# Moving the rows of the first batch so that each half of its load is one contiguous megabyte

## The chip, the cores and the metric

The kernel runs on one NeuronCore of a Trainium2 chip. In profiles DVE is VectorE, ACT is ScalarE, POOL is GpSimd and SP is SyncE, which here only issues transfers. The time is the device time of a run in microseconds. All ratios below are the mean time of one kernel's fast runs over the mean time of the other's fast runs in the same rounds, so they are not quite the ratios of the medians that stand beside them.

## The reference

A masked softmax over the last axis. Each batch has one length, and columns from that length on become zero.

```python
batch, heads, seq_q, seq_k = 16, 8, 256, 256
x       # float32, 16 x 8 x 256 x 256, 2 MB for each batch
lengths # 128 to 255, one for each batch

for b in range(batch):
    length = lengths[b]
    masked = x[b, :, :, :length]
    masked = masked - np.max(masked, axis=-1, keepdims=True)
    e = np.exp(masked)
    result[b, :, :, :length] = e / np.sum(e, axis=-1, keepdims=True)
```

The rows of a batch are independent of each other and share a length. A row may therefore sit in any partition, as long as it is stored where it came from.

## The kernel before

Each batch is 2048 rows of 1 KB. Partition p holds the 16 rows 16p to 16p + 15, so its share is 16 KB that are contiguous in memory.

```python
x_f = x.rearrange("b h q k -> b (h q) k").rearrange("b (p t) k -> b p t k", p=P)
out_f = ...  # the same for the output
slots, ahead = 8, 4            # 8 batches in SBUF, the first 4 loaded by SP

# SP: batch 0 in two halves (8 of each partition's 16 rows), then batches 1 to 3 whole
for h in range(2):
    s = slice(h * half, (h + 1) * half)
    nc.sync.dma_start(out=xt[:, 0, s], in_=x_f[0, :, s]).then_inc(s_ld[h], 16)
for b in range(1, ahead):
    nc.sync.dma_start(out=xt[:, b], in_=x_f[b]).then_inc(s_ld[b + 1], 16)

# SP: stores, the first not before the third half has been exponentiated
nc.sync.wait_ge(s_exp, 3)
for b in range(batch):
    for s in parts(b):         # batch 0 in one piece, most others in two or three
        nc.sync.wait_ge(s_out, 2 * b + (s.stop - 1) // half + 1)
        # ... (a wait from batch 2 on is cut)
        nc.sync.dma_start(out=out_f[b, :, s, :], in_=xt[:, b % slots, s, :])  # ...

# GpSimd: loads of batches 4 to 15, only the columns that are needed, in a loop
nc.gpsimd.wait_ge(s_ld[ahead - 1], 16)         # batch 2 has landed
# ... wait for the slot's store; pick a width; start the load

# VectorE: clip (the mask) and divide; ScalarE: exp with row sums
def mask(b, s): ...    # waits for the load: for batch 0, for each half by itself
def divide(b, h): ...  # waits for exp; reciprocal, then multiply
mask(0, slice(0, half))
mask(0, slice(half, nt))
```

The softmax here doesn't subtract the row's maximum and nothing guards it: scores larger than these inputs give would overflow.

## Time and profile before

| | before |
|---|---|
| median of 4 runs | 156.16 us (155.84 to 156.23) |
| span in the profile | 154.7 us |
| busy share of DVE / ACT | 75% / 68% |
| time of DMA packets, per DMA engine | 151.4 us |
| DVE's first clip starts at | 6.60 us |
| first store issued at | 19.86 us |

The lines are shown in the prediction. The page gives busy shares and forty slices of the span. The timeline gives start, length, engine, source line and operation of each instruction. The stretches give busy times, the DMA share and the rate in GB/s. A stretch counts a packet whole where it starts, so its rate is rough by a packet for each engine. Beside these, the trace has a record of each DMA packet: its queue, start, size and duration. In SP's queue one packet carries one partition's contiguous run; GpSimd's packets here have 1280 to 16384 B.

The **packet sum** is the time of all packets of both data queues, divided by 16 engines. The **excess** of a transfer is what its packets took over their usual 611 ns (16384 B) or 309 ns (8192 B), summed and divided by 16; where a stretch holds GpSimd's packets, each is compared with what its size usually takes, and only differences between kernels count there. A **landing** is the end of a transfer on one of the 16 engines, and the **spread** is the time between the first landing and the last. The **MB by 24 us** spread each packet's bytes evenly over its time.

The prediction and the expectations count packet times from a zero 0.13 us before that of the timeline, and in the MB by 24 us they count each started packet whole (8.93 MB for the kernel before). The text below uses the timeline's zero.

### The profile page before, as it was taken

How to read it: one execution, taken by the hardware profiler on the slowest of the kernel's cores; microseconds unless marked ns; L12 is line 12 of the kernel's file. 1: busy time of each engine (PE TensorE's matmuls, PEld its weight loads, DVE VectorE, ACT ScalarE, POOL GpSimd, SP SyncE). 2: the span in 40 equal slices, each digit the busy share in tenths (PEclk: the TensorE clock that was granted, in tenths of full speed). 3: DMA queues.
4: the chain of work that ended last, by engine and by line, in shares of the span. 5: the costliest groups of instructions: out<-in, count | busy, mean ns of one | idle time of the engine just before them, and what ended most of it. 6: DMA issues, size and time to landing. Idle time of an engine off the chain costs nothing.

```text
span 154.7 us, 1324 instructions
## 1 busy us (share of the span) xinstructions
PE 0.2 (0%) x1; PEld 0.1 (0%) x1; DVE 115.7 (75%) x84; ACT 105.2 (68%) x514; POOL 19.0 (12%) x25
## 2 busy tenths in 40 slices
PE   0000000000000000000000000000000000000000
PEld 0000000000000000000000000000000000000000
DVE  1249999952999696979979696969689629796700
ACT  3087799992692959778695959595976906959200
POOL 4910031000220110201111020202001000000000
DMA  4999999999999999999999999999999999999992
GB/s 116 426 449 424 428 398 406 398 407 447 400 410 395 402 409 414 415 417 411 404 424 407 417 408 409 415 416 416 416 417 419 419 448 415 426 445 419 430 421 85
DMA packets 9988, 62.08 MB, mean 401 GB/s; under 512 B 850, under 2 KB 946, under 8 KB 6274
## 3 DMA queue, kind: packets, MB, share of 16 engines
q1 hardware_dynamic: 5904, 41.95, 65.8%
q0 software_dynamic: 4080, 20.12, 32.1%
q14 instruction: 2, 0.02, 0.0%
q10 hardware_dynamic: 2, 0.00, 0.0%
HBM read 28.51 MB, written 33.55 MB: 401 GB/s over the span
## 4 chain that ended last, share of the span: by engine, by line
DMA 55%; DVE 19%; ACT 8%; issue 8%; ACTq 2%; SPq 1%; POOLq 1%; DVEq 0%
DMA xt<-in_x_dram 34%; DMA out_dram<-xt 21%; DVE xt L222 9%; DVE xt L195 9%; ACT xt L252 8%; ACTq L252 2%; DVE inv_sum L219 1%; SPq L109 1%; POOLq L99 0%; SPq L111 0%; SPq L120 0%; DVEq L212 0%; POOLq L135 0%; POOLq L130 0%; ACTq L247 0%
## 5 line engine op out<-in xcount | busy, mean ns | idle before, releaser
L252 ACT ACTIVATE xt<-xt x256 | 102.4, 401 | 37.2 <-DVE xt L195 37.2
L222 DVE TENSOR_TENSOR xt<-xt,inv_sum 128x2048 f32<-128x2048 f32 x32 | 73.4, 2292 | 1.1
L252 ACT ACTIVATION_READ_ACCUMULATOR xt<-xt x256 | 47.9, 187 | 0.0
L195 DVE SCALAR_TENSOR_TENSOR xt<-down,len_s,xt 128x2048 f32<-128x2048 f32 (+1 forms) x17 | 37.8, 2222 | 13.1 <-DMA xt<-in_x_dram 13.0
L130 POOL DMA_DIRECT2D xt<-in_x_dram x12 | 12.8, 1064 | 95.5 <-issue 50.6
L219 DVE RECIPROCAL inv_sum<-row_sum 128x8 f32<-128x8 f32 x32 | 6.3, 198 | 14.4 <-ACT xt L252 14.4
L149 POOL MEMSET xt<- 128x1536 f32 x4 | 5.3, 1386 | 1.1 <-DVE len_s L186 1.1
L244 ACT ACT_TABLE_LOAD x1 | 1.3, 1283 | 1.6 <-SPq L81 1.6
L178 DVE TENSOR_SCALAR down<-iota_i 128x256 f32<-128x256 int32 x1 | 0.3, 297 | 1.6 <-POOL iota_i L141 1.6
L183 DVE CAST len_b<-word 1x16 bf16<-1x16 int32 x1 | 0.2, 163 | 0.4 <-DMA word<-in_lengths_dram 0.4
L186 DVE TENSOR_SCALAR len_s<-len_f 128x16 f32<-128x16 f32 x1 | 0.2, 174 | 0.3 <-PE len_f L165 0.3
L141 POOL IOTA iota_i<- 128x256 int32 x1 | 0.3, 331 | 0.6 <-SPq L81 0.6
L146 POOL MEMSET seed<- 1x1 f32 x2 | 0.3, 162 | 0.0
L244 ACT ACTIVATE warm<-const-float32-0.0 128x1 f32<-128x1 f32 x1 | 0.2, 203 | 0.0
L144 POOL MEMSET ones<- 1x128 bf16 x1 | 0.2, 194 | 0.0
L165 PE MATMUL len_f<-len_b,ones 1*128 1x16 bf16 x1 | 0.2, 164 | 2.6 <-DVE len_b L183 2.6
L275 POOL MEMSET const-float32-0.0<- 128x1 f32 x1 | 0.1, 98 | 0.3 <-issue 0.3
L165 PEld LDWEIGHTS len_f<-len_b,ones 1*128 1x128 bf16 x1 | 0.1, 99 | 2.6 <-POOL ones L144 2.6
L275 POOL MEMSET const-float32-1.0<- 128x1 f32 x1 | 0.1, 98 | 0.0
L275 POOL MEMSET const-bfloat16-1.0<- 128x1 bf16 x1 | 0.1, 98 | 0.0
L275 POOL MEMSET const-uint8-127<- 128x1 uint8 x1 | 0.1, 98 | 0.0
L275 POOL BASE_LOAD x1 | 0.0, 17 | 0.1
## 6 DMA issues: line engine op xcount, KB each, us to landing
out_dram<-xt SPq DMA_DIRECT2D x19, 1024.0 KB
out_dram<-xt SPq DMA_DIRECT2D x14, 512.0 KB
xt<-in_x_dram SPq DMA_DIRECT2D x3, 2048.0 KB, 16.1
out_dram<-xt SPq DMA_DIRECT2D x3, 2048.0 KB
xt<-in_x_dram POOLq DMA_DIRECT2D x3, 1728.0 KB, 16.9
xt<-in_x_dram POOLq DMA_DIRECT2D x2, 2048.0 KB, 18.5
xt<-in_x_dram POOLq DMA_DIRECT2D x2, 1600.0 KB, 16.8
xt<-in_x_dram POOLq DMA_DIRECT2D x2, 1280.0 KB, 14.8
```

The costliest lines, as they stand in the source:

```text
L109: nc.sync.dma_start(out=xt[:, 0, s], in_=x_f[0, :, s]).then_inc(s_ld[h], 16)
L130: nc.gpsimd.dma_start(out=xt[:, slot, :, :w], in_=x_n[:, n, :, :w]).then_inc(s_sw[par], 16)
L141: nc.gpsimd.iota(iota_i, pattern=[[1, seq_k]], base=0, channel_multiplier=0).then_inc(s_iota, 1)
L146: nc.gpsimd.memset(seed[:, par : par + 1], 0.0).then_inc(s_st[par], 64)
L149: nc.gpsimd.memset(xt[:, b, :, low:], 0.0).then_inc(s_fill, 1)
L165: nc.tensor.matmul(len_f, lhsT=ones, rhs=len_b, start=True, stop=True).then_inc(s_lenf, 1)
L195: return nc.vector.scalar_tensor_tensor(out=t, in0=down[:, None, lo:hi].to_broadcast([P, s.stop - s.start, hi - lo]), scalar=len_s[:, b : ...
L219: step(nc.vector.reciprocal(out=inv_sum[:, b, s], in_=row_sum[:, b, s]))
L222: nc.vector.tensor_tensor(out=t, in0=t, in1=inv_sum[:, b, s, None].to_broadcast([P, half, seq_k]), op=ALU.mult,).then_inc(s_out, 1)
L244: nc.scalar.activation(out=warm, in_=nc.const_aps.tensor(0.0, (P, 1), F32), func=EXP)
L252: ins = nc.scalar.activation(out=e, in_=e, func=EXP, accum_out=sum_h[:, bass.ds(i, 1), j])
L275: nc = _bacc.Bacc("TRN2", target_bir_lowering=False, num_devices=1)
```

## The change

The intent is an earlier first half. Partition p now holds rows 8p to 8p + 7 of the first megabyte and rows 8p to 8p + 7 of the second, so each half of the load is one contiguous megabyte. The store must put the rows back, so it writes two runs of 8 KB per partition instead of one of 16 KB.

```diff
+    x_0 = x[0].rearrange("h q k -> (h q) k").rearrange("(u p t) k -> p u t k", u=2, p=P)
+    out_0 = out[0].rearrange("h q k -> (h q) k").rearrange("(u p t) k -> p u (t k)", u=2, p=P)
...
-            nc.sync.dma_start(out=xt[:, 0, s], in_=x_f[0, :, s]).then_inc(s_ld[h], 16)
+            nc.sync.dma_start(out=xt[:, 0, s], in_=x_0[:, h]).then_inc(s_ld[h], 16)
...
-                nc.sync.dma_start(
-                    out=out_f[b, :, s, :], in_=xt[:, b % slots, s, :]
-                ).then_inc(s_b, 16 * ((s.stop - s.start) // quarter))
+                if b == 0:
+                    to = out_0
+                    at = xt[:, b, s, :].rearrange("p (u t) k -> p u (t k)", u=2)
+                else:
+                    to = out_f[b, :, s, :]
+                    at = xt[:, b % slots, s, :]
+                nc.sync.dma_start(out=to, in_=at).then_inc(s_b, 16 * ((s.stop - s.start) // quarter))
```

## The prediction

> **What bounds the kernel now.** I read the page's busy shares first, then the queues, then the end of the chain, then the first ten microseconds, because the change touches only the first batch.
>
> Busy shares, the forty slices and the queues of the kernel before:
>
> ```profile
> PE 0.2 (0%) x1; PEld 0.1 (0%) x1; DVE 115.7 (75%) x84; ACT 105.2 (68%) x514; POOL 19.0 (12%) x25
> ...
> DMA  4999999999999999999999999999999999999992
> ...
> DMA packets 9988, 62.08 MB, mean 401 GB/s; under 512 B 850, under 2 KB 946, under 8 KB 6274
> ...
> q1 hardware_dynamic: 5904, 41.95, 65.8%
> q0 software_dynamic: 4080, 20.12, 32.1%
> ```
>
> No compute engine is over 75% busy, and the DMA row is at 9 from the second slice to the last but one. The two queues' packets took 65.8% + 32.1% = 97.9% of 16 engines' span, 0.979 x 154.7 = 151.5 us for each DMA engine. The packets start 2.2 us after the span begins and end near 152, so the DMA engines are never without work. The time is a start of 2.2 us, some 150 us of packets, and a tail of under 3 us in which the last semaphores arrive and the program closes.
>
> The stretches at the end (length; busy time and instruction counts of PE, PEld, DVE, ACT, POOL; clock; DMA share; GB/s):
>
> ```profile
> 20.00:140.00 120.00, 0.00 (x0) 0.00 (x0) 99.11 (x70) 89.68 (x445) 12.77 (x12) 1.00 1.02 414
> ...
> 148.00:150.00 2.00, 0.00 (x0) 0.00 (x0) 0.00 (x0) 0.00 (x0) 0.00 (x0) 1.00 1.05 442
> 150.00:151.00 1.00, 0.00 (x0) 0.00 (x0) 0.00 (x0) 0.00 (x0) 0.00 (x0) 1.00 0.97 410
> 151.00:152.00 1.00, 0.00 (x0) 0.00 (x0) 0.00 (x0) 0.00 (x0) 0.00 (x0) 1.00 0.53 221
> ```
>
> The last division ends at 144.33 + 2.29 = 146.6 us, yet the engines carry on at full rate until about 151.3. That is 4.7 us; the last store is 1 MB, which at 414 GB/s takes 2.5 us. So some 2 us of older stores stood in front of it. The compute chain has about 2 us of slack at the end: the end is set by the sum of packet times. A change counts if it alters that sum, or leaves the engines without work.
>
> Now the beginning (start, length, engine, line, operation):
>
> ```profile
> 1.13 0.86 SPq L109 DMA_DIRECT2D xt<-in_x_dram  x2
> ...
> 6.60 1.28 DVE L195 SCALAR_TENSOR_TENSOR xt<-down,len_s,xt 128x1024 f32<-128x1024 f32 x1 [3.61 <-DMA xt<-in_x_dram]
> ...
> 9.05 1.29 DVE L195 SCALAR_TENSOR_TENSOR xt<-down,len_s,xt 128x1024 f32<-128x1024 f32 x1 [1.16 <-DMA xt<-in_x_dram]
> ...
> 19.86 8.20 SPq L120 DMA_DIRECT2D out_dram<-xt  x4
> ```
>
> The halves of batch 0 reach the DVE 9.05 - 6.60 = 2.45 us apart. A megabyte in 2.45 us is 1.049 MB / 2.45 us = 428 GB/s: the second half already comes at the full rate, with its 8 KB out of every 16 KB. Batch 0's store is issued at 19.86, when the loads of batches 1 to 3 still stand in the queue.
>
> The trace also has a record of each DMA packet. In the SP queue each partition's contiguous run is one packet: 8192 B for the two halves (256 packets), 16384 B for loads and stores of whole batches, 8192 or 4096 B for stores in parts. Their times, on one DMA engine:
> - first 64 packets of batch 0 (four on each engine): mean 457 ns, up to 1275; the other 192: 309 to 318 ns.
> - loads of batches 1 and 2, 16384 B: all 256 of them exactly 611 ns.
> - 8192 B stores later on: medians 309 to 315 ns. All of these write 8 KB out of every 16 KB too.
> - batch 0's store, 128 packets of 16384 B: median 612, mean 651, up to 1140 ns.
>
> **What the Trainium skill says.** Its page "DMA: Bandwidth & Descriptors", section "Bandwidth", part "Where 436 GB/s comes from", puts the ceiling of the 16 engines at 435 GB/s. The trace agrees: 428 GB/s here, 16 x 8192 B / 309 ns = 424, and 16 x 16384 B / 611 ns = 429. There is next to nothing left for a better address pattern. The same section, "Why small descriptors are slow (HBM only)", states a fixed cost of some 3 cycles for a packet. The trace shows one of that kind: 2 x 309 - 611 = 7 ns for one more packet.
> The section "Latency and other measured facts" says that large power-of-two distances between the partitions' rows in HBM cost rate: 207 GB/s per direction at 512 KiB, 164 at 2 MiB, against 214. The new store has runs one megabyte apart, so this bears on it, but within each megabyte the partitions are 8 KB apart; nothing in the trace of before tests it. The section "Queues, rings and completion order" says that an engine takes turns between queues packet by packet, which matters for one rival below.
>
> **The change part by part.**
> 1. Loads. Each half remains 128 runs of 8192 B, spread over the same 16 engines. Only the HBM addresses move: runs one after another instead of every other run. Packets removed or added: none. Expected at 309 ns each: no difference. What could be saved is the slow opening, (457 - 309) x 4 = 592 ns per engine. I think this belongs to starting, not to the stride: the 192 packets after it have the same stride and go at 309, and batches 1 and 2 enter memory never touched before at 611 from the first packet. I put the expected gain at 0.1 us of those 0.59.
> 2. Store. Each partition's 16 KB now goes to two places, so 128 packets of 16384 B become 256 of 8192 B: eight more packets on each engine. At 2 x 309 - 611 = 7 ns per pair, or 2 x 313 - 611 = 15 ns with the later stores' median, it costs 8 x 7 to 8 x 15 ns = 0.06 to 0.12 us per engine. This lies in the sum that sets the end, so it counts in full.
> 3. Issue. The store's instruction describes twice the runs, perhaps a few tenths of a microsecond more on SP (its issues take a median of 374 ns now). It is issued at 19.86, and its first packet starts at 22.67 behind the loads: 2.8 us in which that is hidden.
> 4. Compute. Rows move to other partitions, but all rows of a batch share one length: same instructions, same shapes. Nothing changes.
> Sum: -0.1 + 0.1 = 0, with a few tenths of noise: 156.19 becomes about 156.2.
>
> **The rivals.**
> - The first half comes sooner. For it: the first packets' 457 ns, and that a contiguous megabyte is half the address range. Against it: the even 309 right after. Full success would take 0.59 us off the start; since the engines have work from then on, all of it could reach the end: 155.6, 0.4% faster. It can't make 2%.
> - The store of two streams a megabyte apart runs badly. For it: the skill's row pitches, and batch 0's store already showing some slow packets. Against it: only two such streams, and 16 engines well spread within them. At the skill's loss for 2 MiB, 214/164, the store's 2.10 MB / 414 GB/s = 5.07 us would become 6.6 us: 157.7, still the same. Only half rate, +5.1 us, would make 161 and count as slower. I give that about one chance in a hundred.
> - The queues' turns shift. Batch 4's load, issued by GpSimd at 20.85, had its first packets only from 26.6, when batch 0's store was nearly through, and DVE then sat idle for 4.42 us until 37.62. Store packets of half the size let that load in with smaller steps, so it may land sooner by something like half a microsecond. The DVE's idle time shrinks by as much, but the packets' sum is the same, and the compute has slack at the end: 156.2 again, perhaps 0.2 either way from a different order of stores and loads.
> - The first division and the first store start earlier, so that loads into reused slots are let go earlier. It needs the first rival, and the DMA engines have no gap that it could fill: nothing.
>
> **Range and chances.** The runs of before span 155.84 to 156.23. The small effects add up to between -0.6 and +0.4; another chip or another day may add 0.3. I predict 156.2, with 155.5 to 157.0 for eight in ten. Two per cent is 3.1 us: a gain of that size has no source in a change that touches 4 of 62 MB already at 98% of the engines' peak, and a loss needs the store at about 60% of its rate. Chances: 0.005 faster, 0.98 same, 0.015 slower.
>
> **What would show it right or wrong.** Right: 128 more packets, about 10116; the SP queue's share of the span within 0.3 points of 65.8%; DVE's first clip within 0.3 us of 6.60 and the second 2.4 to 2.5 us after it; packets of batch 0's store at 309 to 315 ns in the median. Step 1 is wrong if the first 64 packets fall well below 457 ns, or the later 192 rise above 309. Step 2 is wrong if the store's packets take over 330 ns in the mean. The whole would be wrong if a gap opened in the DMA row, or if the end followed the last division without the 4.7 us of stores after it: then compute would be the bound, and the first half's landing would count.

## The result, and the profile after

The changed kernel takes 156.29 us in the median of 4 runs (156.15 to 156.57), and the kernel before 156.16. The ratio is 1.0014, with a 95% interval of 0.9994 to 1.0035: the same.

The page of the changed kernel, busy shares, DMA row, packets and queues:

```profile
PE 0.2 (0%) x1; PEld 0.1 (0%) x1; DVE 115.8 (75%) x84; ACT 105.2 (68%) x514; POOL 19.0 (12%) x25
...
DMA  3999999999999999999999999999999999999992
...
DMA packets 10116, 62.08 MB, mean 401 GB/s; under 512 B 850, under 2 KB 946, under 8 KB 6274
...
q1 hardware_dynamic: 6032, 41.95, 65.9%
q0 software_dynamic: 4080, 20.12, 32.1%
```

There are 128 packets more, all in the SP queue. The bytes, the instructions and the shares are otherwise those of before.

Stretches of the changed kernel at the end (columns as in the prediction):

```profile
20.00:140.00 120.00, 0.00 (x0) 0.00 (x0) 98.05 (x70) 88.19 (x437) 12.77 (x12) 1.00 1.02 414
...
150.00:151.00 1.00, 0.00 (x0) 0.00 (x0) 0.00 (x0) 0.00 (x0) 0.00 (x0) 1.00 0.99 418
151.00:152.00 1.00, 0.00 (x0) 0.00 (x0) 0.00 (x0) 0.00 (x0) 0.00 (x0) 1.00 0.83 352
```

The rate in the long middle is 414 GB/s as before, and the transfers run into the 152nd microsecond again. The opening differs, though. The timeline of the changed kernel:

```profile
1.13 0.86 SPq L113 DMA_DIRECT2D xt<-in_x_dram  x2
...
6.24 1.28 DVE L203 SCALAR_TENSOR_TENSOR xt<-down,len_s,xt 128x1024 f32<-128x1024 f32 x1 [3.24 <-DMA xt<-in_x_dram]
8.69 1.28 DVE L203 SCALAR_TENSOR_TENSOR xt<-down,len_s,xt 128x1024 f32<-128x1024 f32 x1 [1.17 <-DMA xt<-in_x_dram]
...
19.53 8.26 SPq L130 DMA_DIRECT2D out_dram<-xt  x4
```

Both halves are clipped 0.36 us earlier than before (6.60 and 9.05), and the first store is issued 0.33 us earlier (19.86). The last division, in the same timeline:

```profile
145.46 2.29 DVE L230 TENSOR_TENSOR xt<-xt,inv_sum 128x2048 f32<-128x2048 f32 x1
```

It ends at 147.8 us, 1.1 us later than before, and the transfers go on after it.

The span has not become shorter. So where did the third of a microsecond go? The stretches around that first store, first of the kernel before:

```profile
20.00:22.00 2.00, 0.00 (x0) 0.00 (x0) 1.97 (x3) 2.00 (x11) 1.15 (x1) 1.00 1.08 418
22.00:24.00 2.00, 0.00 (x0) 0.00 (x0) 1.97 (x3) 2.00 (x11) 0.14 (x1) 1.00 0.92 360
```

and of the changed kernel:

```profile
20.00:22.00 2.00, 0.00 (x0) 0.00 (x0) 1.97 (x3) 2.00 (x11) 1.29 (x1) 1.00 1.11 401
22.00:24.00 2.00, 0.00 (x0) 0.00 (x0) 1.97 (x3) 2.00 (x11) 0.00 (x0) 1.00 0.85 299
```

Both kernels dip here, the changed one deeper. With each packet's bytes spread over its time, the rates from 22 to 24 us are 374 and 328 GB/s, a smaller gap than the stretches' 360 and 299. By 24 us the changed kernel has moved 8.72 MB against 8.85 MB: 0.13 MB, or 0.31 us at 414 GB/s. I then had four things to settle. Is the earlier landing real or luck? Is the deeper dip real, and what makes it? And what is a microsecond at the opening worth at the end?

### The profile page after: what moved, and what is told of

The parts are those of the page before. It is cut to its first block, busy times and chain, and to the rows that moved or that the text cites. A ratio compares the mean times of both kernels' runs of the same rounds, so it can differ in the third digit from the quotient of the medians.

```text
span 154.7 us, 1324 instructions
## 1 busy us (share of the span) xinstructions
PE 0.2 (0%) x1; PEld 0.1 (0%) x1; DVE 115.8 (75%) x84; ACT 105.2 (68%) x514; POOL 19.0 (12%) x25
## 4 chain that ended last, share of the span: by engine, by line
DMA 55%; DVE 20%; ACT 8%; issue 8%; ACTq 2%; SPq 2%; POOLq 1%; DVEq 0%
DMA xt<-in_x_dram 34%; DMA out_dram<-xt 20%; DVE xt L230 10%; DVE xt L203 9%; ACT xt L260 8%; ACTq L260 2%; SPq L130 1%; DVE inv_sum L227 1%; SPq L113 1%; POOLq L103 0%; SPq L115 0%; DVEq L220 0%; POOLq L143 0%; POOLq L138 0%; ACTq L255 0%
```

## The experiments

Twelve kernels ran. The calls' medians of the kernel before, over 11 runs each, were 156.27, 156.02 and 156.05 us. Kernels that change only one side of batch 0 store its rows in a wrong order.

**Theories.** A: the addresses make no difference, and what the two traces show is chance. B: contiguous runs land earlier, and the store gives it back.

### Both kernels again

No edit.

> The kernel before, unchanged, to see how far the opening and the middle move by themselves. Theory A (the addresses make no difference; the 0.36 us by which the first clip came earlier in the changed kernel, and the 0.13 MB by which its DMA engines were behind from 24 us on, are chance): the first clip starts anywhere in 6.2 to 6.7 us, and the bytes moved by 24 us anywhere in 8.7 to 9.0 MB. Theory B (the contiguous load lands earlier, and the store in two pieces gives it back): the first clip at 6.6 again within 0.1, and 8.9 MB moved by 24 us. Ratio 1.000 within 0.002 in both.

> The changed kernel, unchanged. Theory A: as for the kernel before, the first clip anywhere in 6.2 to 6.7 us and 8.7 to 9.0 MB moved by 24 us; ratio 1.000 to 1.001. Theory B: the first clip at 6.24 again within 0.1, the mean of the first 64 packets near 412 ns, 8.74 MB by 24 us; ratio 1.000 to 1.002, since gain and loss cancel.

The kernel before took 156.19 us (ratio 0.9995, 0.9975 to 1.0014) and the changed kernel 156.17 us (ratio 0.9997, 0.9971 to 1.0023). The change is worth nothing that 6 runs can see. The first clip of the kernel before, repeated:

```profile
6.52 1.28 DVE L195 SCALAR_TENSOR_TENSOR xt<-down,len_s,xt 128x1024 f32<-128x1024 f32 x1 [3.53 <-DMA xt<-in_x_dram]
```

and of the changed kernel, repeated:

```profile
6.17 1.28 DVE L203 SCALAR_TENSOR_TENSOR xt<-down,len_s,xt 128x1024 f32<-128x1024 f32 x1 [3.19 <-DMA xt<-in_x_dram]
```

The 0.35 us are there again, and so is the dip: 8.86 MB by 24 us in the kernel before and 8.76 MB in the changed one. Theory A loses its main point.

### The loads alone, and the store alone

```diff
# loads_only and loads_again: the new loads, the store as before
-                if b == 0:
+                if False:
                     to = out_0
# store_only: the loads as before, the new store
-            nc.sync.dma_start(out=xt[:, 0, s], in_=x_0[:, h]).then_inc(s_ld[h], 16)
+            nc.sync.dma_start(out=xt[:, 0, s], in_=x_f[0, :, s]).then_inc(s_ld[h], 16)
```

> Contiguous first loads, the store as before (the rows of batch 0 are then stored in a wrong order; on purpose). Theory A: ratio 1.000 within 0.001, time as before. Theory B: first clip at 6.24, 8.93 MB or more by 24 us, and the 0.2 to 0.4 us of the opening reach the end: ratio 0.9975 to 0.9990.

> First loads as before, batch 0's store in two runs per partition a megabyte apart (wrong order of rows; on purpose). Theory A: eight more packets per DMA engine at 7 to 15 ns, so 0.06 to 0.12 us: ratio 1.0004 to 1.0008. Theory B: first clip at 6.6, a loss of 0.3 to 0.5 us between 22 and 24 us that the load does not make up: ratio 1.002 to 1.003.

> Only the loads changed, a second time (wrong order of rows on purpose). The first try gave 0.9982, 95% interval 0.9962 to 1.0002. The delay of 1.1 us at the first clip cost 0.45 us at the end, so by the same slope 0.33 us gained there would be worth 0.14 us. Theory G (a part of the gain reaches the end): ratio 0.998 to 0.9995. Theory N (nothing reaches it): 0.9995 to 1.001. The first clip at 6.15 to 6.35 us in both.

| kernel | median us | ratio (95%) | first clip, us | MB by 24 us | excess of batch 3's load, us |
|---|---|---|---|---|---|
| loads only | 155.94 | 0.9982 (0.9962 to 1.0002) | 6.23 | 8.74 | 0.53 |
| loads only, again | 156.20 | 1.0002 (0.9987 to 1.0018) | 6.23 | 8.72 | 0.65 |
| store only | 156.23 | 0.9992 (0.9971 to 1.0013) | 6.50 | 8.84 | 0.38 |

The earlier clip comes with the loads. So does the deeper dip, and theory B had put it on the store: B's second half is wrong as stated. The time moves with neither. The first try of the loads alone looked like a gain, the second did not, so any gain is below what these runs resolve, about 0.2%.

The store's own cost is in its packets. Their mean was 331, 325 and 329 ns in the three profiles with the new store and normal timing (changed kernel, its repeat, store only). The packets of 16384 B of batch 0's store took 651 and 642 ns in the two profiles of the kernel before. With sixteen small packets against eight large ones per engine, that is 16 x 331 - 8 x 651 = 88 ns, and 16 x 325 - 8 x 642 = 64 ns for the repeats. In the two kernels of the next section but one, where no load of GpSimd runs beside this store, the means are 309.0 and 611.0 ns: 16 x 309 - 8 x 611 = 56 ns. The median small packet took 309 ns, the same as in a load, so two streams a megabyte apart do no harm.

### Runs farther apart

```diff
+    x_w = x[0:2].rearrange("b h q k -> (b h q) k").rearrange("(p t) k -> p t k", p=P)
-            nc.sync.dma_start(out=xt[:, 0, s], in_=x_f[0, :, s]).then_inc(s_ld[h], 16)
+            nc.sync.dma_start(out=xt[:, 0, s], in_=x_w[:, s]).then_inc(s_ld[h], 16)
```

> The kernel before, with each partition of the first two loads taking 8 KB out of every 32 KB (rows of batch 1 among them, so batch 0's output is wrong on purpose). In the six profiles so far the spread of the 16 engines' landings of the first half was 0.90, 0.78, 0.74 us with 8 of 16 KB and 0.46, 0.24, 0.34 us with contiguous runs; the mean landing was 5.57 to 5.64 us in all six. Theory B1 (the distance between runs makes some engines lose more than others in the first rounds): spread 0.7 us or more and the first clip at 6.5 or later. Theory A1 (what helps is only that a contiguous megabyte starts alike on all engines by some other chance): spread anywhere from 0.2 to 0.9, first clip 6.1 to 6.7.

> Runs of 8 KB out of every 32 KB, a second time (wrong on purpose), now timed. The first look had the first clip at 6.14 us and a spread of 0.44 us. If the distance of 16 KB is what is bad: first clip under 6.4 and spread under 0.7 again, and a time like that of the contiguous loads, 0.997 to 0.9995. If the first look was luck: first clip 6.5 or later.

The single look took 155.81 us (state unknown), the timed repeat 155.97 us (ratio 0.9992, 0.9979 to 1.0006). The clip in the first look:

```profile
6.14 1.28 DVE L197 SCALAR_TENSOR_TENSOR xt<-down,len_s,xt 128x1024 f32<-128x1024 f32 x1 [3.16 <-DMA xt<-in_x_dram]
```

In the repeat it came at 6.20. The spread of the landings was 0.44 and 0.52 us, and the mean landing 5.29 and 5.30 us, earlier than in any other kernel (5.44 to 5.55). So a greater distance between runs is not worse, and theory B1 falls: contiguity isn't what makes the last landing early. Of the three patterns tried, it is 8 KB out of every 16 KB whose last engine lands late. Why that one does, and what other distances do, no run shows.

### GpSimd's first load held back

GpSimd's instruction for batch 4's load begins at 20.4 to 20.9 us and lasts 1.3 us, just where the dip is, so it was a suspect.

```diff
         nc.gpsimd.wait_ge(s_ld[ahead - 1], 16)
+        nc.gpsimd.wait_ge(s_ld[ahead], 16)
```

> The kernel before, with GpSimd's first load held until batch 3 has landed (about 24 us instead of 18.8). Theory P (the slow packets at 21 to 23 us come from GpSimd's descriptor writing for batch 4's load, which starts at 20.5 to 20.9): the excess over the packets' floor between 20 and 24 us falls from 0.35 us per engine to under 0.1. Theory W (they come from the change from reads to writes, when the first store's packets enter): it stays at 0.3 or more. Time within 0.3 us of the kernel before in both, since batch 4's load did not move before 26.6 us anyway.

> The changed kernel with the same hold. Theory P: excess between 20 and 24 us falls from 0.63 us per engine to under 0.15, bytes moved by 24 us rise from 8.76 to 8.9 MB or more, batch 3's mean landing from 23.27 to 23.0 us. Theory W: 0.5 us or more stays, and 8.7 to 8.8 MB. Time within 0.3 us of the kernel before in both.

GpSimd's first load in the kernel before with the hold:

```profile
26.97 1.29 POOL L130 DMA_DIRECT2D xt<-in_x_dram  x1 [18.60 <-issue]
```

GpSimd is now far from the dip, but the excess between 20 and 24 us stays: 0.38 us with the old loads (0.35 and 0.38 without the hold) and 0.61 us with the new ones (0.64 and 0.65). Theory P is wrong for that stretch. It was right about a smaller piece: between 24 and 28 us, the excess of 0.24 and 0.17 us of the kernel before went to 0.00. It came back later, where the held load now was: 0.7 us more between 28 and 36 us than in the kernel before.

My expectation for the time was wrong. The holds took 157.07 us (1.0066, 1.0048 to 1.0083) and 157.42 us (1.0085, 1.0064 to 1.0106). I had argued that batch 4's load didn't move before 26.6 us anyway. But it had to wait behind what SP had queued before it. Issued at 26.97 instead of 20.85, its first packet came at 32.3 instead of 26.5, and batch 4's clip at 41.41 instead of 37.62.

### The first clip delayed

The 0.34 us can be taken the other way: let the landing be as it is, and delay the clip with a VectorE operation into a spare tile.

```diff
+        nc.vector.wait_ge(s_ld[0], 16)
+        for r in range(1):       # slow_1us: 1 x 128x1024; slow_4us: 2 x 128x2048
+            dn = down[:, None, :].to_broadcast([P, 4, seq_k])
+            nc.vector.tensor_tensor(out=spare[:, r], in0=dn, in1=dn, op=ALU.max)
         mask(0, slice(0, half))
# after_delayed: the same in the changed kernel, 1 x 128x256
```

> The kernel before with one more VectorE operation of about 1.2 us (128x1024) between the landing of the first half and the first clip: three times the 0.34 us that the change gained there, in the other direction. Theory S (the first landing is not on the path, because the first store's packets come 2.8 us after its issue behind the loads): the first clip 1.2 us later, the first store issued near 21.0 instead of 19.86, the first packet of it still at 22.7, time within 0.2 us of the kernel before, ratio 0.999 to 1.001. Rival R (each microsecond at the opening is one at the end): ratio 1.006 to 1.008.

> The kernel before with two VectorE operations of about 2.3 us each (128x2048) before the first clip, so some 4.4 us of delay. Theory S (there is slack of about 1.6 us, the 2.8 us between the first store's issue and its first packet less the 1.2 us that a store takes from issue to packet; past it every microsecond counts): 4.4 - 1.6 = 2.8 us, ratio 1.016 to 1.020. Theory L (a steady 0.4 us for each microsecond, as the smaller delay showed): 1.8 us, ratio 1.010 to 1.013. Rival R (all of it): 1.027 to 1.029.

> The changed kernel with one VectorE operation of about 0.44 us (128x256) before the first clip, so that the 0.34 us gained in the landing is used up again: the first clip near 6.55, the first store's issue near 19.85. Theory I (batch 3's load is slowed because the store is issued earlier beside it): its excess over the packets' floor falls from 0.55 to 0.58 us per engine to 0.25 to 0.4, as in the kernel before, and 8.85 to 8.95 MB are moved by 24 us. Theory E (it is slowed because the 16 engines run more evenly with contiguous loads and meet the change to writes together): it stays at 0.5 or more, and 8.75 MB. Time within 0.3 us of the kernel before in both.

The small delay in the kernel before, timeline and then stretches:

```profile
6.44 1.23 DVE L233 TENSOR_TENSOR spare<-down 128x1024 f32<-128x1024 f32 x1 [3.45 <-DMA xt<-in_x_dram]
7.58 1.28 DVE L196 SCALAR_TENSOR_TENSOR xt<-down,len_s,xt 128x1024 f32<-128x1024 f32 x1
...
20.82 14.34 SPq L121 DMA_DIRECT2D out_dram<-xt  x7
```

```profile
20.00:22.00 2.00, 0.00 (x0) 0.00 (x0) 2.00 (x2) 2.00 (x11) 1.13 (x1) 1.00 1.01 434
22.00:24.00 2.00, 0.00 (x0) 0.00 (x0) 1.97 (x2) 2.00 (x11) 0.72 (x2) 1.00 1.06 426
```

The dip between 20 and 24 us is all but gone (434 and 426 GB/s). GpSimd's load is still at its old place; batch 0's clips, exponentials, divisions and store have moved. Batch 3's load then has no excess at all. The same delay tool in the changed kernel, whose loads are contiguous:

```profile
6.13 0.43 DVE L240 TENSOR_TENSOR spare<-down 128x256 f32<-128x256 f32 x1 [3.15 <-DMA xt<-in_x_dram]
6.98 1.28 DVE L204 SCALAR_TENSOR_TENSOR xt<-down,len_s,xt 128x1024 f32<-128x1024 f32 x1 [0.42 <-issue]
...
20.23 14.04 SPq L131 DMA_DIRECT2D out_dram<-xt  x7
```

It delayed the clip by more than I meant, 6.98 - 6.24 = 0.74 us, since 0.42 us of issue came on top. Its excess in batch 3's load is 0.15 us, below the 0.25 to 0.4 of theory I as the delay was larger than planned, and 8.95 MB are moved by 24 us. Theory E wanted 0.5 us or more. Sorted by the time at which SP issues the first store:

| kernel | store issued at, us | excess of batch 3's load, us |
|---|---|---|
| wide runs, two looks | 19.41, 19.45 | 0.79, 0.71 |
| changed, two looks | 19.44, 19.53 | 0.58, 0.57 |
| loads only, two looks | 19.50, 19.51 | 0.65, 0.53 |
| changed, GpSimd held | 19.65 | 0.61 |
| store only | 19.78 | 0.38 |
| before, two looks | 19.82, 19.86 | 0.30, 0.28 |
| before, GpSimd held | 19.96 | 0.38 |
| changed, delayed 0.7 us | 20.23 | 0.15 |
| before, delayed 1.1 us | 20.82 | 0.00 |
| before, delayed 4.1 us | 23.87, after the load's end | 0.00 |

The earlier the first store is issued, the longer it stands beside loads that are still running, and the slower those go. In every kernel with a dip, the first slow packet of batch 3's load (over 630 ns) came 0.9 to 1.8 us after the store's issue, before the store's own packets began. The delays are interventions, so that the timing of batch 0's chain sets the excess is shown. They move batch 0's compute together with its store; that it is the store's issue is argued from those 0.9 to 1.8 us, as no run moves the store alone. How a waiting store would slow the reads isn't shown either.

**What a delay costs.** The small one took 156.58 us: 1.0029 (1.0009 to 1.0049), so 0.0029 x 156 = 0.45 us for a clip about 1.05 us later. Theory S, of a slack that swallows it, had a bound of 1.001 and is wrong; so is rival R. The large one took 157.51 us: 1.0090 (1.0072 to 1.0108), so 1.4 us for a clip about 4.1 us later (10.63 us against 6.5). Theory L asked for 1.010 to 1.013, so it is nearly right, and S (1.016 or more) and R (1.027 or more) are out. The changed kernel with its delay of 0.74 us took 156.51 us: 1.0026 (1.0009 to 1.0043); I had expected less than 0.3 us of difference. So a microsecond of delay at the opening cost some 0.35 to 0.55 us at the end. The intervals of the two smaller delays are wide (from 0.1 to 0.7 us and from 0.2 to 0.9 us for each microsecond); the large one gives 0.27 to 0.41.

That the DMA engines have hardly a gap did not make the end deaf to the opening. One reason is that the packet sum isn't fixed. It was 151.44 and 151.58 us in the two profiles of the kernel before, 152.00 with the small delay and 152.44 with the large one. The small delay's 0.5 us appeared after 24 us: some 0.4 us more excess between 24 and 30 us than in the kernel before, and 0.25 us more between 40 and 60 us. The sum isn't all of it. In the changed kernel with its delay it was 151.57 us, against 151.58 and 151.56 without, and yet the runs were slower: the time ends with the last engine, whose last data packet ended at 153.33 us there and at 153.18 and 152.80 without. With the large delay, the first store came so late that GpSimd's load ran alone. Stretches of that kernel:

```profile
22.00:24.00 2.00, 0.00 (x0) 0.00 (x0) 2.00 (x2) 2.00 (x11) 0.56 (x1) 1.00 0.72 185
...
26.00:28.00 2.00, 0.00 (x0) 0.00 (x0) 1.97 (x3) 2.00 (x11) 0.00 (x0) 1.00 0.92 199
```

The engines look 72% and 92% busy and move about 200 GB/s (229 and 204 with the bytes of each packet spread over its time): a DMA share near 0.9 is no proof of full rate. Between 20 and 30 us this kernel's engines were also idle for 0.6 us in the mean, so its loss is packet time and gaps together. Its last division:

```profile
139.64 2.29 DVE L223 TENSOR_TENSOR xt<-xt,inv_sum 128x2048 f32<-128x2048 f32 x1
```

It was done at 141.9 us, 4.7 us earlier than in the kernel before, and the run was slower all the same: the loss lies in the transfers.

## Why the prediction was right or wrong

The time, the range and the class were right: 156.29 us against 156.2, inside 155.5 to 157.0. (The 156.19 that it starts from is one of the four runs; their median is 156.16.) Step by step:

- **The bound.** The packets do fill the span: span less packet sum lay between 2.6 and 3.8 us in all fourteen profiles. The end did not follow the last division, which ended at 146.6 us before, at 147.8 in the changed kernel and at 141.9 with the large delay. But the packets don't "end near 152": that is the mean engine of the kernel before (151.8), and the last one went on to 153.0. What was wrong is the step from the packet sum and the compute chain's slack to an opening that is harmless. The fourth rival, that an earlier first division and store are worth "nothing", failed in the direction that was tested: delays at the first clip reached the end at about 0.4 us for each microsecond. That a gain is worth as much is not shown.
- **Step 1, the loads.** I put down 0.1 us of gain. In packet time it was about that: the first 64 packets had a mean of 468 ns over six profiles with the old loads (450 to 486) and 434 ns over six with contiguous ones (412 to 505), so 34 x 4 = 136 ns per engine. But the landing is not the mean engine; DVE waits for the last one: the last count of the semaphore came at 6.34 us before and at 5.98 in the changed kernel, and the clips began at 6.60 and 6.24. The mean landing of the 16 engines stayed (5.50 us against 5.48), and their spread fell from 0.56 to 1.03 us to 0.24 to 0.71 us. The semaphore's last count came at 5.99 us in the mean of the six instead of 6.29: 0.30 us. Here the two groups do not overlap (6.12 to 6.43 and 5.92 to 6.06). The limit that I had set for the clip, within 0.3 us of 6.60, was missed by 0.06 in the changed kernel's profile. "This belongs to starting, not to the stride" was half right: the slow start is in every kernel, but how unevenly it falls on the engines depends on the addresses.
- **Step 2, the store.** I estimated 0.06 to 0.12 us, and measured 0.06 to 0.09 us by packet means. My sign for failure, a mean over 330 ns, was met by 1 ns in the first profile. It was badly chosen: half of a large packet of before is already 651 / 2 = 326 ns.
- **Step 3, the issue, and step 4, the compute.** Both as said: the store's issue was hidden, and busy times are equal. (By the timeline's zero, the first packet of batch 0's store in the kernel before came at 22.5 us, 2.6 us after its issue, and not at 22.67.)
- **The rivals.** The first half does come sooner, by half of what that rival allowed. The store a megabyte apart runs at the usual 309 ns. The queues' turns shifted as guessed: batch 4's clip came at 37.09 and 36.88 us instead of 37.62 and 37.36, half a microsecond, and the store alone gave 36.98. It is seen nowhere in the time.

The sum: 0.30 us earlier, at some 0.4 us for each microsecond if a gain counts as a delay does, is a gain of about 0.1 us, and the eight extra packets cost 0.06 to 0.09 us. One thing goes against an early gain: with contiguous loads batch 3's load has some 0.3 us more excess. The two terms are both below what the runs resolve, so that they cancel is worked out from profiles, not measured as a time. That the first term came out at the 0.1 us of the prediction is partly luck: I had a small gain that counts in full, and the profiles show a gain three times as large of which some four tenths would arrive.

## What to carry to other kernels

An engine waits for the last of sixteen DMA engines, so look at the spread of their landings as well as at the mean. An idle-free DMA row doesn't make the end independent of what happens early: issue times can decide which transfers run beside each other, and how long their packets take. To get a first idea of what an early gain could be worth, delay that place on purpose by a few times the gain; here delays of 1 and 4 us cost about 0.4 us for each, so three tenths of a microsecond could bring a tenth.

## What the Trainium skill lacked or had wrong

- "DMA: Bandwidth & Descriptors", "Queues, rings and completion order", has the engines take turns between queues packet by packet. If the trace's packets are those of the page, this differs: a newly issued transfer waited until the other queue's earlier transfer was well under way. Batch 4's load, issued at 20.85, had its first packet at 26.5 us behind the store of SP that was issued a microsecond before. With the large delay it was the other way round: the store issued at 23.87 had its first packet at 28.0 us, with only GpSimd's packets in between, where SP's very first load took 1.1 us. Only then did packets of both queues start side by side. A packet of the page may hold several descriptors, and the records don't show which of them belong together.
- The same page, "Latency and other measured facts", gives row pitches of 512 KiB and more. It has nothing on small pitches at the start of a program: 8 KB runs 16 KB apart spread the engines' first landings over 0.56 to 1.03 us, contiguous ones over 0.24 to 0.71 us, and runs 32 KB apart over 0.44 and 0.52 us.
- No page says that loads slow down while a store is issued beside them and before its own packets start: 0.00 us of excess in batch 3's load when the store was issued at 20.82, and 0.79 us when at 19.41. That the store is the cause is argued, not shown.

